# The first tile's output projection split into high and low weight parts, with the convolution's norm between them

## The chip, the cores and the metric

The kernel runs on one core of one Trainium2 chip. The core has five engines with instruction streams of their own: PE (TensorE, matmuls and transposes), DVE (VectorE), ACT (ScalarE), POOL (GpSimd) and SP (SyncE, which here only issues DMAs). They wait for one another by semaphores. Each engine takes its instructions in the order in which the built program lists them. The metric is the device time of one execution in microseconds.

## The reference, cut to what matters

Two decoder layers over 256 positions of width 1024. Each layer is a half-step SwiGLU block, a pair of token mixers side by side, and a second half-step SwiGLU block, each between two RMS norms. All is float32. The mixer pair of layer 0, on which the change acts, is

```python
proj = h @ w_in                                   # 1024 -> q, k, v, ga, gb of 512 each
q, k, v, ga, gb = jnp.split(proj, ...)
o_a = moba_attention(rope(q), rope(k), v)         # causal softmax attention here
hconv = ga * jax.nn.sigmoid(gb)
hconv = depthwise_causal_conv(hconv, conv_w, 31) + conv_b
mu = mean(hconv, -1); var = mean((hconv - mu) ** 2, -1)
o_b = silu((hconv - mu) * rsqrt(var + 1e-5) * ln_g + ln_b)
m = jnp.concatenate([o_a, o_b], -1) @ w_out       # 1024 -> 1024
x = x + rmsnorm(m, g[3])
f = swiglu(rmsnorm(x, g[4]), ffn_w_gate[layer, 1], ...)
```

Layer 1 has a gated mixer and a stick-breaking attention in the same place, with an input projection of the same kind.

## The kernel before, in words

**Tiles.** The 256 positions are two tiles of 128 (t = 0, 1). Activations that enter a matmul are transposed, so that the channel is the partition; weights move through PE in pieces of 128 rows by 512 columns.

**High and low parts.** PE multiplies a rounded form of float32 (F32R). To keep float32's accuracy every operand is two parts: ACT copies it rounded (the high part, L106 for weights, L167 for activations), and DVE subtracts that from the original (the low part, L107, L168). A product is three matmuls (`mm3`, L155 to L157): high by high, the activation's high by the weight's low, the activation's low by the weight's high. Weight blocks of 1 MB are loaded by SP into one of five buffers (`raw`, L88) and split into nine buffers each for high and low (`hi`, `lo`). A `raw` buffer is free for the next load once its second low part is made; a `hi` or `lo` buffer once the last matmul has read it.

**Scheduler.** The kernel is traced in program order, and a list scheduler then sets each engine's order, by readiness in its own model and by program order as priority. `tc.issue_after(ins)` ties instructions of a block behind `ins` on its engine. The list `fence` holds such anchors for the weight splits (L97 to L100).

**The mixer of layer 0** (`even_mixer`). Ten projections `ab` run over chunks and tiles (`turns`). The convolution's 31 taps run on POOL (0 to 12, `side_taps`) and DVE (13 to 30, `conv`, L620, into PSUM) beside the attention, and L623 adds both sums into `cacc`. `conv_norm` is a chain over all engines: PE means over channels (`cmean`, L628), DVE centres (L629), ACT squares (`csq`, L631), PE sums (`cvar`, L635), DVE and POOL make the inverse root (L637, L638), DVE puts it on a diagonal (`dg`, L642), PE spreads it (`crstd`, L644), DVE scales (L645), ACT applies silu (L649) and rounds (`xh_oT`, L651), DVE makes the low part (`xl_oT`, L652). The output projection has two halves of the weights' rows: `out_part(t, 0)` takes rows 0 to 511 (blocks `abo0`, `abo1`) with the attention's output, `out_part(t, 1)` takes `abo2`, `abo3` with the convolution's. Each is 24 matmuls into `m_t_0` and `m_t_1`. The program order is `conv`, `out_part(0, 0)`, `conv_norm` (tied behind the last matmul of it), `out_part(1, 0)`, `out_part(0, 1)`, `out_part(1, 1)`.

**After it.** When a tile's `m` is complete its `tail` runs: ACT squares it (`j_l0f`, L256), DVE and POOL make the factor, DVE updates `x` (L263), ACT squares and scales `x` (L201, `y_l0f`, L212), PE transposes (`xT_l0f`), DVE multiplies by the gain (`a_l0f`, L216), ACT and DVE split it, and the SwiGLU's first products (`gu`) follow. The SwiGLU then runs in blocks (`M`, L366 to L368) whose first DVE step (L390) subtracts two loaded blocks `raw_b`.

**The norm ahead of a mixer** (`pre_norm`). For t = 1 it gives back a function: the sums of squares come at once, but the transposes `xT`, the gain (L231) and the split come only when the first projection of tile 1 calls it (`in_proj`).

Of the kernel before, what the change touches and what calls it, by code (L numbers as in the profile page):

```python
# [49 lines left out]
def trunk(ctx, tc, x, norm_g, w_gate, w_up, w_down, ab_in, ab_out, conv_w, conv_b, conv_g, conv_bb,  # L50
# [170 lines left out]
    def pre_norm(t, gi, name):  # L221

        s = sp.tile([P, 2], F32, tag="rs", name=f"s2_{name}{t}", bufs=4)

        def parts():
            hi, lo = xT_tiles(t, name) if gi else [sp.tile([P, KD, P], F32R, tag=tag, name=f"{tag}_{name}{t}", bufs=1) for tag in (("S1", "S2"), ("S3", "tg"))[t]]
            for j in range(2):
                ps = transposes(xs[t][:, j * 512:(j + 1) * 512], f"xT{j}_{name}{t}")
                y = sp.tile([P, 512], F32, tag="y", name=f"y{j}_{name}{t}", bufs=2)
                gk = gT[:, gi * KD + 4 * j:gi * KD + 4 * j + 4, None].to_broadcast([P, 4, P])  # L230
                nc.vector.tensor_tensor(y.rearrange("p (a b) -> p a b", b=P), ps.rearrange("p (a b) -> p a b", b=P), gk, op=ALU.mult)  # L231
                split(y, hi[:, 4 * j:4 * j + 4].rearrange("p a b -> p (a b)"), lo[:, 4 * j:4 * j + 4].rearrange("p a b -> p (a b)"))
            return hi, lo

        def rstd():
            for j in range(2):
                c = slice(j * 512, (j + 1) * 512)
                junk = sp.tile([P, 512], F32, tag="y", name=f"j2{j}_{name}{t}", bufs=2)
                nc.scalar.activation(junk, xs[t][:, c], AF.Square, scale=PRE_SCALE, accum_out=s[:, j:j + 1])
            return rstd_of(s, 1e-6, f"p{name}{t}")  # L240
# [754 lines left out]
```

## Time and profile before

| | us |
|---|---|
| runs | 993.72, 995.27, 996.56 |
| median | 995.27 |
| the profiled execution | 995.27 |
| its span, first to last instruction | 993.5 |
| PE busy | 958.0 (96%) |
| PE weight loads busy | 764.0 (77%) |
| DVE busy | 829.0 (83%) |
| ACT busy | 582.6 (59%) |

The profiled execution has the time of the median, so a sum against it is a sum against the median; 1.8 us lie outside its span. All times below are microseconds from the span's start. A row of a timeline gives the start, the length from the first to the last of its instructions, the engine, the line, the output and the inputs, and in brackets how long the engine had been idle before it and what ended that. Matmuls overlap, so the distance from one start to the next is what one costs. The granted clock is a share of 2.4 GHz; 0.50 is the lower level, 1.2 GHz.

### The profile page before, as it was taken

The page shows a single profiled execution, that of the slowest core. Times are in us where ns is not written, and L with a number is a line of the kernel's source. Part 1 is how long each engine was busy: PE and PEld are TensorE (multiplying, and loading weights), DVE is VectorE, ACT ScalarE, POOL GpSimd, SP SyncE. Part 2 cuts the span into 40 slices and gives each one's busy share as a digit, 9 for nine tenths or more (in the row PEclk, how much of TensorE's full clock was granted, in tenths as well). Part 3 has the DMA queues.
Part 4 walks back from the last instruction along what each step waited for, and adds up shares of the span by engine and source line. Part 5 has one row for each costly group of instructions (what it writes and reads, how often), then busy time and mean ns, then how long its engine had stood idle before and what let it go on. Part 6 is the DMA issues. An engine that isn't in the chain of part 4 may idle for free.

```text
span 993.5 us, 11867 instructions
## 1 busy us (share of the span) xinstructions
PE 958.0 (96%) x4357; PEld 764.0 (77%) x4358; DVE 829.0 (83%) x1014; ACT 582.6 (59%) x863; POOL 91.0 (9%) x97
## 2 busy tenths in 40 slices
PE   7999999999978899999999999999999999999997
PEld 5777888778756688888777878877787778788875
DVE  6999999679867699999788999996657479999983
ACT  7575656557525566566575755565555477647561
POOL 0100000039930000000000000000000010000000
PEclk9999999999979999999999999999999999999999
DMA  9656657447015328393862566485565042749241
GB/s 316 220 175 219 205 177 274 159 146 268 1 58 187 96 85 280 127 314 99 304 211 86 171 210 224 157 294 173 170 233 169 18 153 85 222 160 302 90 180 43
DMA packets 121755, 175.33 MB, mean 176 GB/s; under 512 B 4481, under 2 KB 96321, under 8 KB 121696
## 3 DMA queue, kind: packets, MB, share of 16 engines
q1 hardware_dynamic: 121536, 174.50, 52.9%
q8 instruction: 34, 0.56, 0.2%
q14 instruction: 25, 0.20, 0.1%
q10 hardware_dynamic: 160, 0.07, 0.0%
HBM read 173.50 MB, written 1.05 MB: 176 GB/s over the span
## 4 chain that ended last, share of the span: by engine, by line
PE 81%; DVE 9%; ACT 3%; DMA 3%; issue 2%; POOL 1%; SPq 0%; POOLq 0%; DVEq 0%; ACTq 0%
PE f L155 7%; PE f L157 7%; PE f L156 7%; PE gu L155 6%; PE gu L157 6%; PE gu L156 6%; PE gX L366 4%; PE gX L367 4%; PE gX L368 4%; PE gY L366 3%; PE gY L367 3%; PE gY L368 3%; PE ab L155 2%; DVE lo_gu L107 2%; PE ab L157 2%
## 5 line engine op out<-in xcount | busy, mean ns | idle before, releaser
L155 PE MATMUL f<-hi_dn,hs 128*128 128x512 f32 x352 | 139.9, 402 | 1.6 <-ACT hs L167 1.4
L156 PE MATMUL f<-lo_dn,hs 128*128 128x512 f32 x352 | 138.3, 393 | 0.5 <-DVE lo_dn L107 0.5
L157 PE MATMUL f<-hi_dn,hs 128*128 128x512 f32 x352 | 138.0, 393 | 0.4 <-DVE hs L168 0.4
L106 ACT ACTIVATE hi_t<-raw_b 128x1024 fp32r<-128x1024 f32 x96 | 98.0, 1054 | 67.0 <-DVE raw_b L406 49.1
L107 DVE TENSOR_TENSOR lo_t<-raw_b,hi_t 128x1024 fp32r<-128x1024 f32 x96 | 114.2, 1220 | 14.6 <-ACT hi_t L106 14.6
L106 ACT ACTIVATE hi_dn<-raw_dn 128x1024 fp32r<-128x1024 f32 x88 | 91.2, 1055 | 35.3 <-PE gu L157 18.0
L107 DVE TENSOR_TENSOR lo_dn<-raw_dn,hi_dn 128x1024 fp32r<-128x1024 f32 x88 | 105.7, 1219 | 5.7 <-ACT hi_dn L106 5.5
L107 DVE TENSOR_TENSOR lo_gu<-raw_gu,hi_gu 128x1024 fp32r<-128x1024 f32 x80 | 96.1, 1219 | 9.7 <-ACT hi_gu L106 9.6
L106 ACT ACTIVATE hi_gu<-raw_gu 128x1024 fp32r<-128x1024 f32 x80 | 83.3, 1054 | 19.0 <-DMA raw_gu<-in_ffn_w_up_dram 5.0
L107 DVE TENSOR_TENSOR lo_b<-raw_b,hi_b 128x1024 fp32r<-128x1024 f32 x72 | 86.4, 1219 | 1.1 <-ACT hi_b L106 1.1
L106 ACT ACTIVATE hi_b<-raw_b 128x1024 fp32r<-128x1024 f32 x72 | 74.0, 1054 | 20.0 <-PE gu L157 15.1
L155 PEld LDWEIGHTS f<-hi_dn,hs 128*128 128x128 f32 x352 | 65.6, 188 | 18.2 <-ACT hs L167 5.4
L157 PEld LDWEIGHTS f<-hi_dn,hs 128*128 128x128 f32 x352 | 66.1, 188 | 15.9 <-DVE hs L168 2.5
L156 PEld LDWEIGHTS f<-lo_dn,hs 128*128 128x128 f32 x352 | 66.2, 188 | 15.2 <-DVE lo_dn L107 2.7
L167 ACT ACTIVATE hs<-hT 128x256 fp32r<-128x256 f32 x88 | 32.4, 379 | 66.1 <-PE hT L163 66.0
L155 PE MATMUL gu<-hi_gu,xh_l1f 128*128 128x512 f32 x160 | 63.2, 396 | 0.0
L156 PE MATMUL gu<-lo_gu,xh_l1f 128*128 128x512 f32 x160 | 62.7, 392 | 0.2 <-DVE lo_gu L107 0.2
L157 PE MATMUL gu<-hi_gu,xl_l1f 128*128 128x512 f32 x160 | 61.7, 391 | 0.6 <-DVE xl_l1f L168 0.6
L168 DVE TENSOR_TENSOR hs<-hT,hs 128x256 fp32r<-128x256 f32 x88 | 36.1, 419 | 17.2 <-ACT hs L167 16.6
L366 PE MATMUL gY<-hi_t,S 128*128 128x512 f32 x96 | 38.7, 403 | 0.0
L368 PE MATMUL gY<-hi_t,S 128*128 128x512 f32 x96 | 37.9, 395 | 0.0
L367 PE MATMUL gY<-lo_t,S 128*128 128x512 f32 x96 | 37.8, 394 | 0.0
(365 smaller groups left out, 2222.8 us busy)
## 6 DMA issues: line engine op xcount, KB each, us to landing
raw_dn<-in_ffn_w_down_dram SPq DMA_DIRECT2D x44, 1024.0 KB, 5.1
raw_b<-in_ffn_w_gate_dram SPq DMA_DIRECT2D x48, 512.0 KB, 4.2
raw_b<-in_ffn_w_up_dram SPq DMA_DIRECT2D x48, 512.0 KB, 5.7
raw_gu<-in_ffn_w_gate_dram SPq DMA_DIRECT2D x38, 512.0 KB, 4.0
raw_gu<-in_ffn_w_up_dram SPq DMA_DIRECT2D x38, 512.0 KB, 5.1
raw_ab<-in_ab_w_in_dram SPq DMA_DIRECT2D x10, 1024.0 KB, 7.0
raw_cd<-in_cd_w_in_dram SPq DMA_DIRECT2D x10, 1024.0 KB, 5.2
raw_abo<-in_ab_w_out_dram SPq DMA_DIRECT2D x4, 1024.0 KB, 5.1
```

What stands on the lines that cost most here:

```text
L106: nc.scalar.activation(hi, r, AF.Copy)
L107: nc.vector.tensor_tensor(lo, r, f32v(hi), op=ALU.subtract)
L155: nc.tensor.matmul(ps, xh, wh, start=first, stop=False)
L156: nc.tensor.matmul(ps, xh, wl, start=False, stop=False)
L157: return nc.tensor.matmul(ps, xl, wh, start=False, stop=last)
L167: nc.scalar.activation(hi, ps, AF.Copy)
L168: nc.vector.tensor_tensor(lo, ps, f32v(hi), op=ALU.subtract)
L366: nc.tensor.matmul(ps, A[0][:, k, :], wh[:, o], start=first and k == 0, stop=False, **tc_skip)
L367: nc.tensor.matmul(ps, A[0][:, k, :], wl[:, o], start=False, stop=False, **tc_skip)
L368: nc.tensor.matmul(ps, A[1][:, k, :], wh[:, o], start=False, stop=k == 3, **tc_skip)
```

## The change

Three edits. First, `out_part(0, 0)` loads `abo1` with its high parts only, multiplies all four weight pieces of rows 0 to 511 by their high parts (16 matmuls, both activation parts), then traces `conv_norm` tied behind the last of these, then makes the low parts of `abo1` tied behind the centring, and last multiplies by the low parts (8 matmuls). Second, the fence for the splits that follow is the centring at once, and for the splits of the next block it is the last rounding and the last low part of `conv_norm`. Third, `pre_norm` of tile 1 does all its work where it is called, in both layers.

```diff
+    def low_parts(raw, units):
+        with ExitStack() as stack:
+            for ins in fence:
+                stack.enter_context(tc.issue_after(ins))
+            for u, (hi, lo) in enumerate(units):
+                nc.vector.tensor_tensor(lo, raw[:, u * 1024:(u + 1) * 1024], f32v(hi), op=ALU.subtract)
...
             nc.scalar.activation(hi, r, AF.Copy)
-            nc.vector.tensor_tensor(lo, r, f32v(hi), op=ALU.subtract)
+            if low:
+                nc.vector.tensor_tensor(lo, r, f32v(hi), op=ALU.subtract)
             units.append((hi, lo))
-        return units
+        return units if low else (raw, units)
...
-        if t and gi:
-            r = rstd()
-            return lambda: (*parts(), r, None)
-        two = parts()
-        return *two, rstd(), None
+        return hi, lo, rstd_of(s, 1e-6, f"p{name}{t}"), None
...
-                if t == 1:
-                    fence[:] = [scaled.ins, last.ins]
...
-                nc.vector.tensor_tensor(ol[:, 4:8, :], cacc[:, :, o], f32v(oh[:, 4:8, :]), op=ALU.subtract)
+                low = nc.vector.tensor_tensor(ol[:, 4:8, :], cacc[:, :, o], f32v(oh[:, 4:8, :]), op=ALU.subtract)
+            late[:] = [last.ins, low.ins]
...
-            for i in (0, 1) if part == 0 else (2, 3):
+            rows = (0, 1) if part == 0 else (2, 3)
+            for i in rows:
                 if i not in ow:
-                    ow[i] = prep_rows(ab_out[0], 256 * i, f"abo{i}")
-                last = rows_product(t, accs[t], oT[t][0], oT[t][1], (2 * i, 2 * i + 1), ow[i], i == 0, i == 3)
+                    ow[i] = prep_rows(ab_out[0], 256 * i, f"abo{i}", (t, part, i) != (0, 0, 1))
+            if (t, part) == (0, 0):
+                for low in (False, True):
+                    for i in rows:
+                        for j in range(2):
+                            o = slice(j * 512, (j + 1) * 512)
+                            for k in (0, 1):
+                                wh, wl = (ow[i] if low or i == 0 else ow[i][1])[k]
+                                xh, xl = oT[t][0][:, 2 * i + k, :], oT[t][1][:, 2 * i + k, :]
+                                for a, b in ((xh, wl),) if low else ((xh, wh), (xl, wh)):
+                                    ins = nc.tensor.matmul(accs[t][j], a, b[:, o], start=not low and i + k == 0 and a is xh, stop=False)
+                    if not low:
+                        with tc.issue_after(ins.ins):
+                            fence[:] = [conv_norm().ins]
+                        low_parts(*ow[1])
+                        ow[1] = ow[1][1]
+                return
+            for i in rows:
+                rows_product(t, accs[t], oT[t][0], oT[t][1], (2 * i, 2 * i + 1), ow[i], i == 0, i == 3)
...
         conv()
-        with tc.issue_after(out_part(0, 0).ins):
-            centred = conv_norm()
+        out_part(0, 0)
         out_part(1, 0)
-        late = fence[:]
-        fence[:] = [centred.ins]
         out_part(0, 1)
         fence[:] = late
         out_part(1, 1)
```

The scheduler's orders show it. Names carry buffer numbers here, and line numbers of the changed kernel are some nine higher up to the norm (L164 to L166 are `mm3`, L703 the new loop). In names such as `m0_0_1` the last two figures are the tile and the column half, and `lo1_abo0` is the second low part of block `abo0`.

PE around the mean of `conv_norm`, before:

```order
L156 MATMUL m0_0_0_2599<-lo1_abo1_2630,xh0_oT_2254 128x512
L157 MATMUL m0_0_0_2599<-hi1_abo1_2629,xl0_oT_2255 128x512
L157 MATMUL m0_0_1_2600<-hi0_abo1_2625,xl0_oT_2255 128x512
L155 MATMUL m0_0_1_2600<-hi1_abo1_2629,xh0_oT_2254 128x512
L156 MATMUL m0_0_1_2600<-lo1_abo1_2630,xh0_oT_2254 128x512
L157 MATMUL m0_0_1_2600<-hi1_abo1_2629,xl0_oT_2255 128x512
L628 MATMUL cmean_2645<-cacc_1802,cst_69 128x256 x4
L156 MATMUL m0_1_0_2687<-lo0_abo0_2604,xh1_oT_2343 128x512
L157 MATMUL m0_1_0_2687<-hi0_abo0_2603,xl1_oT_2344 128x512
L155 MATMUL m0_1_0_2687<-hi1_abo0_2607,xh1_oT_2343 128x512
```

The same place after:

```order
L703 MATMUL m0_0_1_2600<-hi0_abo1_2613,xl0_oT_2255 128x512
L703 MATMUL m0_0_1_2600<-hi1_abo1_2616,xh0_oT_2254 128x512
L703 MATMUL m0_0_1_2600<-hi1_abo1_2616,xl0_oT_2255 128x512
L164 MATMUL m0_1_0_2687<-hi0_abo0_2603,xh1_oT_2343 128x512
L164 MATMUL m0_1_1_2688<-hi0_abo0_2603,xh1_oT_2343 128x512
L624 MATMUL cmean_2635<-cacc_1822,cst_69 128x256 x4
L703 MATMUL m0_0_0_2599<-lo0_abo0_2604,xh0_oT_2254 128x512
L703 MATMUL m0_0_1_2600<-lo0_abo0_2604,xh0_oT_2254 128x512
L165 MATMUL m0_1_0_2687<-lo0_abo0_2604,xh1_oT_2343 128x512
L166 MATMUL m0_1_0_2687<-hi0_abo0_2603,xl1_oT_2344 128x512
L164 MATMUL m0_1_0_2687<-hi1_abo0_2607,xh1_oT_2343 128x512
```

Before, the mean stands behind all 24 matmuls of tile 0 and three of tile 1. Now it stands behind the 16 high-part matmuls and two of tile 1; eight of the 16 stand further up, among the last steps of the attention, and the eight low-part matmuls follow behind the mean, mixed with those of tile 1.

DVE from the end of the convolution to the diagonal, before:

```order
L623 TENSOR_TENSOR cacc_1802<-conv1_2524,cside_1803 128x512
L107 TENSOR_TENSOR lo0_abo0_2604<-raw_abo0_2601,hi0_abo0_2603 128x1024
L107 TENSOR_TENSOR lo1_abo0_2608<-raw_abo0_2601,hi1_abo0_2607 128x1024
L107 TENSOR_TENSOR lo0_abo1_2626<-raw_abo1_2623,hi0_abo1_2625 128x1024
L107 TENSOR_TENSOR lo1_abo1_2630<-raw_abo1_2623,hi1_abo1_2629 128x1024
L629 TENSOR_TENSOR cacc_1802<-cacc_1802,cmean_2645 128x1024
L107 TENSOR_TENSOR lo0_abo2_2716<-raw_abo2_2713,hi0_abo2_2715 128x1024
L107 TENSOR_TENSOR lo1_abo2_2720<-raw_abo2_2713,hi1_abo2_2719 128x1024
L637 TENSOR_SCALAR cv4_2662<-cvar_2653 128x2
L107 TENSOR_TENSOR lo0_abo3_2738<-raw_abo3_2735,hi0_abo3_2737 128x1024
```

The same place after:

```order
L619 TENSOR_TENSOR cacc_1822<-conv1_2524,cside_1823 128x512
L116 TENSOR_TENSOR lo0_abo0_2604<-raw_abo0_2601,hi0_abo0_2603 128x1024
L116 TENSOR_TENSOR lo1_abo0_2608<-raw_abo0_2601,hi1_abo0_2607 128x1024
L625 TENSOR_TENSOR cacc_1822<-cacc_1822,cmean_2635 128x1024
L106 TENSOR_TENSOR lo0_abo1_2614<-raw_abo1_2611,hi0_abo1_2613 128x1024
L106 TENSOR_TENSOR lo1_abo1_2617<-raw_abo1_2611,hi1_abo1_2616 128x1024
L633 TENSOR_SCALAR cv4_2652<-cvar_2643 128x2
L116 TENSOR_TENSOR lo0_abo2_2716<-raw_abo2_2713,hi0_abo2_2715 128x1024
L638 TENSOR_SCALAR dg0_2655<-cst_69,cv4_2652 128x128
L638 TENSOR_SCALAR dg1_2666<-cst_69,cv4_2652 128x128
L116 TENSOR_TENSOR lo1_abo2_2720<-raw_abo2_2713,hi1_abo2_2719 128x1024
L641 TENSOR_TENSOR cacc_1822<-cacc_1822,crstd0_2657 128x4x128
```

Before, four low parts stand ahead of the centring; now two, and those of `abo1` stand behind it. All later low parts have moved down by two places in the chain: those of `abo3` now stand behind the scaling (the rows after the last one shown).

PE at the start of the mixer of layer 0, where tile 1's first projection begins, before:

```order
L156 MATMUL ab_0_1_1871<-lo1_ab_3_1_1868,xh0_l0m_1664 128x512
L157 MATMUL ab_0_1_1871<-hi1_ab_3_1_1867,xl0_l0m_1665 128x512
L163 MATMUL hcT0_1898<-cst_69,hc0_1896 128x128 x4
L163 MATMUL xT0_l0m1_1906<-cst_69,x1_68 128x128 x4
L163 MATMUL xT1_l0m1_1915<-cst_69,x1_68 128x128 x4
L155 MATMUL ab_1_0_1924<-hi0_ab_4_0_1806,xh1_l0m_1904 128x512
L156 MATMUL ab_1_0_1924<-lo0_ab_4_0_1807,xh1_l0m_1904 128x512
```

And after, where the transposes `xT0` and `xT1` of tile 1 now stand:

```order
L166 MATMUL ab_0_0_1844<-hi0_ab_4_1_1836,xl0_l0m_1665 128x512
L172 MATMUL xT0_l0m1_1778<-cst_69,x1_68 128x128 x4
L164 MATMUL ab_0_0_1844<-hi1_ab_4_1_1840,xh0_l0m_1664 128x512
L172 MATMUL xT1_l0m1_1787<-cst_69,x1_68 128x128 x4
L165 MATMUL ab_0_0_1844<-lo1_ab_4_1_1841,xh0_l0m_1664 128x512
L166 MATMUL ab_0_0_1844<-hi1_ab_4_1_1840,xl0_l0m_1665 128x512
L164 MATMUL ab_0_0_1844<-hi1_ab_4_1_1840,xh0_l0m_1664 128x512
L165 MATMUL ab_0_0_1844<-lo1_ab_4_1_1841,xh0_l0m_1664 128x512
L166 MATMUL ab_0_0_1844<-hi1_ab_4_1_1840,xl0_l0m_1665 128x512
L916 MATMUL cwT_ps_1803<-cst_69,cw_sb_584 128x31 x4
L917 MATMUL cwT_ps_1803<-cst_69,cv_sb_586 128x12
```

Before, both transposes stand between the last matmul of tile 0's second projection and the first one of tile 1. Now they stand inside tile 0's first projection, and the transposes of the small weights, which stood ahead of it, follow it. Layer 1 has the same move.

## Rows read from the trace of the kernel before

**Rows 1.** The page: the span, then busy us, share and count by engine.

```profile
span 993.5 us, 11867 instructions
...
PE 958.0 (96%) x4357; PEld 764.0 (77%) x4358; DVE 829.0 (83%) x1014; ACT 582.6 (59%) x863; POOL 91.0 (9%) x97
```

**Rows 2.** Stretches: bounds, length, busy us by engine, granted TensorE clock, DMA share, GB/s.

```profile
213.10:216.80 3.70, 2.00 (x14) 1.35 (x13) 2.02 (x3) 1.23 (x2) 1.18 (x2) 1.00 0.00 0
285.50:295.00 9.50, 6.52 (x16) 4.52 (x17) 8.43 (x12) 0.60 (x1) 0.00 (x0) 0.50 0.11 33
311.20:324.40 13.20, 13.07 (x48) 10.02 (x48) 11.68 (x14) 11.16 (x21) 0.54 (x1) 0.87 0.58 198
329.40:345.00 15.60, 15.50 (x66) 12.60 (x67) 7.89 (x13) 4.87 (x11) 0.84 (x2) 0.89 0.13 43
345.00:495.00 150.00, 149.92 (x671) 121.40 (x670) 138.78 (x149) 92.17 (x123) 0.00 (x0) 1.00 0.61 200
707.60:711.50 3.90, 2.11 (x15) 1.40 (x14) 1.98 (x4) 1.32 (x2) 0.00 (x0) 1.00 0.00 0
```

**Rows 3.** PE in order of time: start, length, instruction, idle before it and its releaser.

```profile
281.11 1.10 PE L574 MATMUL po<-va,pts 128*128 128x64 f32 x8 [0.75 <-ACT pts L571]
...
284.02 1.19 PE L574 MATMUL po<-va,pts 128*128 128x64 f32 x8 [1.36 <-ACT pts L571]
...
285.99 1.11 PE L163 MATMUL oT<-cst,o 128*128 128x128 f32 x4 [0.79 <-DVE o L582]
...
291.24 0.80 PE L156 MATMUL m<-lo_abo,xh_oT 128*128 128x512 f32 x1 [2.23 <-DVE lo_abo L107]
...
298.19 1.89 PE L628 MATMUL cmean<-cacc,cst 128*128 128x256 f32 x8
...
302.55 1.95 PE L635 MATMUL cvar<-cst,csq 128*128 128x1 f32 x16
...
306.95 0.60 PE L644 MATMUL crstd<-dg,cst 128*128 128x128 f32 x4
...
311.28 0.50 PE L155 MATMUL m<-hi_abo,xh_oT 128*128 128x512 f32 x1 [3.72 <-ACT xh_oT L651]
...
326.78 1.27 PE L163 MATMUL xT_l0f<-cst,y_l0f 128*128 128x128 f32 x8 [2.43 <-ACT y_l0f L212]
...
329.40 0.79 PE L155 MATMUL gu<-hi_gu,xh_l0f 128*128 128x512 f32 x1 [1.36 <-ACT xh_l0f L167]
...
344.81 0.48 PE L155 MATMUL gu<-hi_gu,xh_l0f 128*128 128x512 f32 x1
```

**Rows 4.** DVE in order of time, the same columns.

```profile
288.77 1.28 DVE L623 TENSOR_TENSOR cacc<-conv,cside 128x512 f32<-128x512 f32 x2
...
289.97 4.62 DVE L107 TENSOR_TENSOR lo_abo<-raw_abo,hi_abo 128x1024 fp32r<-128x1024 f32 x4
...
300.12 1.22 DVE L629 TENSOR_TENSOR cacc<-cacc,cmean 128x1024 f32<-128x1024 f32 x1 [5.53 <-PE cmean L628]
...
307.96 1.28 DVE L645 TENSOR_TENSOR cacc<-cacc,crstd 128x512 f32<-128x512 f32 x2
...
332.72 2.29 DVE L390 TENSOR_TENSOR raw_b<-raw_b,raw_b 128x2048 f32<-128x2048 f32 x1
...
699.77 1.41 DVE L263 SCALAR_TENSOR_TENSOR x<-tg_l1m,v_ql1m,x 128x512 f32<-128x512 f32 x2
```

**Rows 5.** ACT in order of time.

```profile
301.43 1.07 ACT L631 ACTIVATE csq<-cacc 128x1024 f32<-128x1024 f32 x1 [13.69 <-DVE cacc L629]
...
318.94 0.60 ACT L256 ACTIVATE j_l0f<-m 128x512 f32<-128x512 f32 x1 [0.68 <-PE m L157]
...
325.07 1.04 ACT L106 ACTIVATE hi_dn<-raw_dn 128x1024 fp32r<-128x1024 f32 x1
```

**Rows 6.** SP's queue of DMA issues in order of time.

```profile
326.87 0.50 SPq L88 DMA_DIRECT2D raw_b<-in_ffn_w_up_dram  x1
...
353.63 19.40 SPq L88 DMA_DIRECT2D raw_dn<-in_ffn_w_down_dram  x2
```

More of the change, by code (lines that the diff above doesn't have):

```diff
@@ L78, in trunk, with prep @@
     nc.scalar.activation(early, mhalf, AF.Silu)
-    def prep(loads, name):
-        return split_raw(load(loads, name), name)
+    def prep(loads, name, low=True):
+        return split_raw(load(loads, name), name, low)
     def load(loads, name):
@@ L91, in trunk, with split_raw @@
     fence = []
-    def split_raw(raw, name):
+    def split_raw(raw, name, low=True):
         with ExitStack() as stack:
@@ L97, in split_raw, with split_raw_now @@
                 stack.enter_context(tc.issue_after(ins))
-            return split_raw_now(raw, name)
-    def split_raw_now(raw, name):
+            return split_raw_now(raw, name, low)
+    def low_parts(raw, units):
[4 more added lines that the diff above has]
+                nc.vector.tensor_tensor(lo, raw[:, u * 1024:(u + 1) * 1024], f32v(hi), op=ALU.subtract)
+    def split_raw_now(raw, name, low=True):
         units = []
@@ L146, in prep_in, with prep_rows @@
         return [(hi[:, o:o + 512], lo[:, o:o + 512]) for hi, lo in units for o in (0, 512)]
-    def prep_rows(w, r0, name):
+    def prep_rows(w, r0, name, low=True):
         def loads(raw):
@@ L151, in loads @@
             return [(v, w[r0:r0 + 256, :].rearrange("(k p) f -> p k f", p=P))]
-        return prep(loads, name)
+        return prep(loads, name, low)
     def mm3(ps, xh, xl, wh, wl, first, last):
@@ L223, in pre_norm @@
         s = sp.tile([P, 2], F32, tag="rs", name=f"s2_{name}{t}", bufs=4)
[L225 to L240, printed above, removed]
-        if t and gi:
-            r = rstd()
-            return lambda: (*parts(), r, None)
-        two = parts()
-        return *two, rstd(), None
+        hi, lo = xT_tiles(t, name) if gi else [sp.tile([P, KD, P], F32R, tag=tag, name=f"{tag}_{name}{t}", bufs=1) for tag in (("S1", "S2"), ("S3", "tg"))[t]]
@@ new lines, in pre_norm @@
+        for j in range(2):
+            ps = transposes(xs[t][:, j * 512:(j + 1) * 512], f"xT{j}_{name}{t}")
+            y = sp.tile([P, 512], F32, tag="y", name=f"y{j}_{name}{t}", bufs=2)
+            gk = gT[:, gi * KD + 4 * j:gi * KD + 4 * j + 4, None].to_broadcast([P, 4, P])
+            nc.vector.tensor_tensor(y.rearrange("p (a b) -> p a b", b=P), ps.rearrange("p (a b) -> p a b", b=P), gk, op=ALU.mult)
+            split(y, hi[:, 4 * j:4 * j + 4].rearrange("p a b -> p (a b)"), lo[:, 4 * j:4 * j + 4].rearrange("p a b -> p (a b)"))
@@ L248, in post_norm @@
+        for j in range(2):
+            c = slice(j * 512, (j + 1) * 512)
+            junk = sp.tile([P, 512], F32, tag="y", name=f"j2{j}_{name}{t}", bufs=2)
+            nc.scalar.activation(junk, xs[t][:, c], AF.Square, scale=PRE_SCALE, accum_out=s[:, j:j + 1])
+        return hi, lo, rstd_of(s, 1e-6, f"p{name}{t}"), None
     def post_norm(t, acc, g, half, name, last=False):
@@ L495, in in_proj @@
     def in_proj(t, c, units, pre, name):
-        if callable(pre[t]):
-            pre[t] = pre[t]()
         hi, lo = pre[t][0:2]
@@ L644, in conv_norm @@
                 nc.tensor.matmul(pb[:, 0:P], ones, dg, start=True, stop=True)
-                scaled = nc.vector.tensor_tensor(cacc[:, :, o], cacc[:, :, o], pb[:, None, 0:P].to_broadcast([P, 4, P]), op=ALU.mult)
-                if t == 1:
-                    fence[:] = [scaled.ins, last.ins]
+                nc.vector.tensor_tensor(cacc[:, :, o], cacc[:, :, o], pb[:, None, 0:P].to_broadcast([P, 4, P]), op=ALU.mult)
                 for i in range(4):
@@ L680, in even_mixer @@
         ow = {}
+        late = []
         def proj(t, ci):
@@ L692, in out_part @@
                 accs[t] = [ps_acc(f"m0_{t}_{i}", 0) if t == 0 else ps_mm(f"m0_{t}_{i}") for i in range(2)]
-            for i in (0, 1) if part == 0 else (2, 3):
+            rows = (0, 1) if part == 0 else (2, 3)
+            for i in rows:
                 if i not in ow:
-                    ow[i] = prep_rows(ab_out[0], 256 * i, f"abo{i}")
-                last = rows_product(t, accs[t], oT[t][0], oT[t][1], (2 * i, 2 * i + 1), ow[i], i == 0, i == 3)
+                    ow[i] = prep_rows(ab_out[0], 256 * i, f"abo{i}", (t, part, i) != (0, 0, 1))
+            if (t, part) == (0, 0):
+                for low in (False, True):
+                    for i in rows:
+                        for j in range(2):
+                            o = slice(j * 512, (j + 1) * 512)
[12 more added lines that the diff above has]
+                rows_product(t, accs[t], oT[t][0], oT[t][1], (2 * i, 2 * i + 1), ow[i], i == 0, i == 3)
             if part == 1:
                 tail(t, accs[t])
-            return last
         rest = None
```

## The prediction

> **What bounds the kernel now.** I read the page first [rows 1]. PE is busy for 958.0 of 993.5 us, the engine next to it, DVE, for 829.0. PE's idle time is therefore 993.5 - 958.0 = 35.5 us in all, and a change that leaves the number and size of the matmuls alone, as this one does, can gain only from that idle time and from stretches at the lower clock.
>
> Next I read stretches [rows 2]. In the middle of a SwiGLU (345 to 495 us) PE is busy 149.92 of 150.00 us at a clock of 1.00, and a matmul costs 149.92 / 671 = 0.224 us. DVE is busy 138.78 there and so has 11.2 us to spare. In such a stretch PE is the bound, and a head start won ahead of it is carried to the end. Around the convolution's norm it is otherwise: from 285.5 to 295.0 PE is busy for 6.52 of 9.50 us at a clock of 0.50, the lower level, and a matmul row costs 6.52 / 16 = 0.41 us.
>
> Third, PE in order of time tells what it waits for [rows 3]: 0.75 and 1.36 us for the softmax's `pts`, 0.79 for `o`, 2.23 for `lo_abo`, 3.72 for the rounded output of the norm (`xh_oT`), 2.43 for `y_l0f`, 1.36 for `xh_l0f`. The first five are 8.85 us, and a reader should see what they hide: `cacc` is ready at 288.77 + 1.28 = 290.05 [rows 4], yet `cmean` starts at 298.19 [rows 3], 8.1 us later, only because all 24 matmuls of the first half stand ahead of it, and these wait for low parts that DVE makes in 4 x 1.155 us from 289.97 on. ACT idles 13.69 us before `csq` for the same reason [rows 5].
>
> The profiled execution took 995.27 us, the median of the runs, so the sum is made against that (993.5 of span and 1.8 around it).
>
> **The change, part by part.**
>
> *Term 1, tile 1's norm in layer 0.* The transposes `xT0`, `xT1` move in among the matmuls of the first projection. From 213.10 to 216.80 PE is busy for 2.00 of 3.70 us [rows 2], so 1.70 goes if nothing else is late. Tile 1's `x` is old by then, and the gain and the split lie beside some 18 projection matmuls (18 x 0.224 = 4.0 us). The convolution's side taps may start later for it; at worst that moves `cacc` and eats the gain. Bounds 0 and 1.7, and I take -1.7, since every instruction whose wait is removed has its inputs early.
>
> *Term 2, the same in layer 1.* Idle is 3.90 - 2.11 = 1.79 [rows 2]. Here `x` is fresh: its two updates end at 699.77 + 1.41 = 701.2 [rows 4], the half that `xT0` wants some 0.7 sooner, and the moved transposes may wait about 0.4 for it. I take -1.4 (bounds 0 and 1.8).
>
> *Term 3, the projection around the norm.* Eight of the sixteen high-part matmuls now stand inside the attention's last steps, where they fill the waits of 0.75 and 1.36. The wait of 2.23 for `lo_abo` disappears, as high parts need no DVE. `cmean` waits for `cacc` alone: 290.05 instead of 298.19. Then DVE: `lo0_abo0`, `lo1_abo0` stand ahead of the centring and end at 289.97 + 2 x 1.155 = 292.28, while `cmean` is done at 290.05 + 1.89 = 291.94, so the centring starts at 292.3, 0.3 late. `csq` follows after 1.31 (301.43 - 300.12), at 293.6, and `cvar` could start 1.12 after it (302.55 - 301.43), at 294.7. But PE has 15 matmuls between: 291.94 + 15 x 0.224 = 295.3, which is later and so counts. From `cvar` to `crstd` 4.40 and from there to the matmul with `xh_oT` 4.33, as before [rows 3]: 304.0 instead of 311.28, thus -7.2. One low part (1.155) now stands between diagonal and scaling; it fits nearly into the 1.01 (307.96 - 306.95) that DVE waits there anyway.
>
> What is late next is again `xh_oT`: of the 8.85 us some 1.6 stay, up to 3.0 if PE runs its matmuls faster than before. The low parts of `abo1` end at 292.3 + 1.22 + 2 x 1.155 = 295.8 instead of 289.97 + 4.62 = 294.6, and SP's next load into that buffer starts 1.2 later; it holds a block of the SwiGLU, which PE reaches some 25 us after that. Bounds of the term: 5.0, if the clock is at half up to about 291.7 as in the row, so that ten matmuls cost 0.41 instead of 0.224 (1.9 us) and the centring's delay is not caught up; 7.5 with all 0.3 of it caught up.
>
> The Trainium skill, "Perfetto Trace Analysis", section "Matmul Optimizations", says that TensorE scales its power with its use, so that matmuls should run back to back in batches. The row agrees in so far as the clock is 0.50 behind the waits of 0.75, 1.36 and 0.79 [rows 2, 3]. By that rule the eight matmuls packed into these waits would keep the clock up, and the term stays at 7.2; if the row's 0.50 comes back all the same, it is 5.0 and the sum below 986.2.
>
> *Term 4, the tail.* From `j_l0f` at 318.94 [rows 5] to `xT_l0f` at 326.78 [rows 3] the first tile's chain takes 7.84 us, of which PE waits for 2.43. By the new fences one copy with its low part fewer stands in the chain's way on ACT (1.04, as `hi_dn` at 325.07 [rows 5]) and about one on DVE (1.155, of which I count 0.65, as it lies partly beside POOL's step). That is -1.7; bounds 0 and 2.4.
>
> *Term 5.* That work doesn't vanish; a quarter of a low part ends up between `xT_l0f` and the first `gu`, whose wait was 1.36: +0.3 (0 to 0.4).
>
> *Term 6, a new wait.* On DVE the first SwiGLU step L390 now stands between the first tile's last steps and those of tile 1. It needs a block `raw_b` whose load was issued at 326.87 [rows 6], once a low part of `gu` had freed the buffer. That low part has moved back in DVE's order by about as much as the path moves ahead, so I keep 326.9. L390 started at 332.72 [rows 4], so the load lands within 5.85 of its issue, and L390's 2.29 end by 335.0. Behind it queue three short steps, of about 0.5 each (an estimate from the 0.6 to 0.7 that halves of 128 x 512 take in [rows 4]), that lead to tile 1's first `gu`: 336.5. Without the wait it would be 344.81 [rows 3] - 7.2 - 1.7 + 0.3 = 336.2. So +0.3 to +0.4, and I take 0.4. By these terms 8.2 are left at this point.
>
> *Clock.* From 311.20 to 324.40 48 matmuls took 13.07 us at 0.87 [rows 2], 48 x 0.224 = 10.75 at full clock: 2.3 lost. Whether the shorter wait for `xh_oT` still brings the clock down I can't tell: 2.3 either way, value 0. Small new waits in the SwiGLU: value 0, bound 1.5 worse.
>
> Sum: 1.7 + 1.4 + 7.2 + 1.7 - 0.3 - 0.4 = 11.3; 995.3 - 11.3 = 984.0.
>
> **The rivals.**
>
> *Half of it.* The clock stays at 0.50 around the norm (term 3 is 5.0) and the tail's chain is paced by something other than the copies (term 4 is 0): 1.7 + 1.4 + 5.0 - 0.3 - 0.4 = 7.4, so 987.9. For it: the stretch at 0.50 and 0.87 [rows 2]. Against: the moved matmuls fill the very waits ahead of it.
>
> *DVE paces the SwiGLU.* Whatever PE wins ahead of it is given back inside, because DVE has as much to do as before; only the mixers' terms, or the one in layer 1, stay: 1.4 to 3.1, so 992.2 to 993.9. Against it: DVE's 138.78 beside PE's 149.92 in 150 us [rows 2]. For it: PE's weight loads (764.0) are less busy than DVE (829.0) [rows 1]. The Trainium skill, "Perfetto Trace Analysis", section "Identifying the Most-Contended Engine", speaks for this rival: TensorE's matmul time says little, its weight loads' busy share is to be read, so 77% against DVE's 83%, and DVE would be the engine to relieve. The trace here doesn't bear it out in the SwiGLU's stretch, where PE never waits.
>
> *The norm isn't earlier.* `cacc` or the centring moves back with the steps that now stand ahead on DVE or POOL, and the wait for `xh_oT` grows by what that for `lo_abo` loses: terms 1 and 2 remain, 992.2. Against it: `cacc` at 290.05 hangs on nothing that was moved behind it.
>
> *The load behind L390 comes late (slower).* If its issue on SP stands behind another that waits, as the one at 353.63 waited 19.40 [rows 6], it goes out at 326.9 + 19.4 = 346.3, lands at 352.1, L390 ends at 354.4, and tile 1's `gu` starts near 356, 11 later than before; with terms 1 and 2 that is +8, 1003. The whole change turns into a loss once the block lands after 344.81 + 3.1 - 2.29 - 1.5 = 344.1. For it: three DVE steps are blocked by one load, and its buffer is freed later in the order. Against it: in the trace of before that load waited only 0.50 on the queue.
>
> **How the numbers follow.** Forecast 0.64, half of it 0.16, DVE 0.08, norm not earlier 0.04, late load 0.08. A difference under 0.3% (3 us) is about what a measurement of this kernel can't tell from none. The first two are faster (0.80), the next two count as the same (0.12), the last is slower (0.08). Low end: all bounds at their best, 1.7 + 1.8 + 7.5 + 2.4 + 2.3 (clock) - 0.4 = 15.3, 980.0. High end: the rival with half of it, 987.9, made worse by the 1.5 in the SwiGLU and 2.1 of the clock's 2.3, 991.5. Outside lie the last three cases, 0.20.
>
> **What would show it.** Right: `cmean` about 8 us earlier and waiting for `cacc`; no wait for `lo_abo`; one wait of 1.6 to 3 for `xh_oT`, near 304; `xT_l0f` waiting under 1; tile 1's `gu` near 336; no waits in the two mixers' places; PE as busy in the SwiGLU as before. Wrong: more than 14 us from `cmean` to the matmul with `xh_oT`, idle PE inside the SwiGLU, or a wait of over 2 us that ends with L390.

## The result and the profile after

| | before | after |
|---|---|---|
| median of the runs, us | 995.91 | 982.67 |
| ratio, 95% interval | | 0.9871 [0.9852, 0.9889] |
| the profiled execution | 995.27 | 983.43 |
| its span | 993.5 | 981.6 |

By the ratio the change takes 12.8 us (11.1 to 14.7) off 995.9; forecast were 984.0 and 11.3. The page after, beside [rows 1]:

```profile
span 981.6 us, 11876 instructions
...
PE 954.6 (97%) x4358; PEld 763.6 (78%) x4358; DVE 829.2 (84%) x1014; ACT 581.5 (59%) x863; POOL 91.8 (9%) x97
```

PE's idle time fell from 35.5 to 981.6 - 954.6 = 27.0 us; the other 3.4 us of the span are busy time. 2.3 of that lie between the front and the restart with `xh_oT` (68.84 to 66.53), where the granted clock rose from 0.93 to 0.97. DVE works as long as before. Stretches of the changed kernel, with the columns of [rows 2]; the first is the mixer's front, the second the same piece of the SwiGLU as before:

```profile
201.81:231.87 30.06, 30.06 (x144) 24.43 (x142) 24.19 (x30) 17.47 (x24) 15.39 (x14) 1.00 0.60 207
...
345.00:495.00 150.00, 149.92 (x671) 121.18 (x670) 134.80 (x145) 91.52 (x125) 0.54 (x1) 1.00 0.61 200
```

The front has no idle time left, and in the SwiGLU PE is as full as it was: 149.92 us, 671 matmuls. PE around the norm, beside [rows 3]:

```profile
282.87 1.10 PE L570 MATMUL po<-va,pts 128*128 128x64 f32 x8 [0.89 <-ACT pts L567]
284.75 0.66 PE L172 MATMUL oT<-cst,o 128*128 128x128 f32 x4 [0.78 <-DVE o L578]
...
289.13 1.89 PE L624 MATMUL cmean<-cacc,cst 128*128 128x256 f32 x8
...
294.29 1.84 PE L631 MATMUL cvar<-cst,csq 128*128 128x1 f32 x16
...
298.86 0.61 PE L640 MATMUL crstd<-dg,cst 128*128 128x128 f32 x4
...
302.91 0.79 PE L164 MATMUL m<-hi_abo,xh_oT 128*128 128x512 f32 x1 [2.75 <-ACT xh_oT L645]
...
317.00 1.27 PE L172 MATMUL xT_l0f<-cst,y_l0f 128*128 128x128 f32 x8 [1.51 <-ACT y_l0f L221]
319.65 0.79 PE L164 MATMUL gu<-hi_gu,xh_l0f 128*128 128x512 f32 x1 [1.38 <-ACT xh_l0f L176]
...
334.50 0.74 PE L166 MATMUL f<-hi_dn,hs 128*128 128x512 f32 x2 [0.20 <-DVE hs L177]
```

The wait of 0.75 for `pts` and the one of 2.23 for `lo_abo` are gone, those for `pts` (1.36), `xh_oT` (3.72) and `y_l0f` (2.43) are smaller. DVE, beside [rows 4], and POOL, of which [rows 1] give only the sum:

```profile
287.07 1.28 DVE L619 TENSOR_TENSOR cacc<-conv,cside 128x512 f32<-128x512 f32 x2
288.27 2.35 DVE L116 TENSOR_TENSOR lo_abo<-raw_abo,hi_abo 128x1024 fp32r<-128x1024 f32 x2
291.06 1.22 DVE L625 TENSOR_TENSOR cacc<-cacc,cmean 128x1024 f32<-128x1024 f32 x1 [0.44 <-PE cmean L624]
...
314.45 0.21 DVE L200 TENSOR_SCALAR v_pl0f<-s_l0f 128x1 f32<-128x1 f32 x1
314.58 2.35 DVE L116 TENSOR_TENSOR lo_gu<-raw_gu,hi_gu 128x1024 fp32r<-128x1024 f32 x2
...
331.49 2.29 DVE L388 TENSOR_TENSOR raw_b<-raw_b,raw_b 128x2048 f32<-128x2048 f32 x1 [2.27 <-DMA raw_b<-in_ffn_w_up_dram]
```

```profile
311.26 0.54 POOL L201 TENSOR_TENSOR v_ql0f<-v_ql0f,mhalf 128x1 f32<-128x1 f32 x1 [13.24 <-DVE v_ql0f L200]
314.74 1.46 POOL L201 TENSOR_TENSOR v_pl0f<-v_pl0f,mhalf 128x1 f32<-128x1 f32 x1 [2.93 <-DVE v_pl0f L200]
...
324.53 2.59 POOL L201 TENSOR_TENSOR v_pl0f<-v_pl0f,mhalf 128x1 f32<-128x1 f32 x1 [2.79 <-DVE v_pl0f L200]
```

The two low parts stand ahead of the centring, which then waits 0.44 us for PE instead of 5.53. POOL's power step (the inverse root, L201), the same operation on one column, takes 0.54, 1.46 or 2.59 us. It became the point of the second half of the study.

Single executions differ by a few us, so each stage was measured in every trace, as the distance from one marked PE row to the next (us). The marks are `xT_l0m` of tile 0, the second `hcT`, `cmean`, the restart with `xh_oT`, the first and the last `xT_l0f`, the first `xT_l1f`, `xT_l1m`, the first `xT_l1f` behind layer 1's mixer, and the last matmul:

| | front | to cmean | to restart | to xT_l0f | tile 1's xT | SwiGLU | next SwiGLU | layer 1's mixer | last SwiGLU |
|---|---|---|---|---|---|---|---|---|---|
| before | 42.69 | 64.95 | 13.09 | 15.50 | 17.57 | 162.58 | 178.92 | 115.24 | 185.63 |
| before, again | 42.67 | 65.18 | 13.09 | 15.50 | 17.64 | 162.60 | 178.12 | 113.84 | 184.71 |
| after | 40.36 | 57.26 | 13.78 | 14.09 | 18.07 | 163.18 | 179.22 | 112.15 | 184.58 |
| after, again | 40.36 | 55.94 | 13.89 | 12.71 | 18.15 | 163.18 | 178.97 | 112.20 | 184.72 |
| norm early only | 40.38 | 66.41 | 13.08 | 16.02 | 17.64 | 162.65 | 177.89 | 111.84 | 184.65 |
| projection only | 42.71 | 57.09 | 13.78 | 12.69 | 17.69 | 163.20 | 177.70 | 113.85 | 184.63 |
| quarters | 40.34 | 55.96 | 12.41 | 15.53 | 18.80 | 163.17 | 178.45 | 111.82 | 184.74 |
| last version | 40.36 | 55.94 | 12.42 | 12.41 | 17.72 | 164.10 | 178.03 | 111.89 | 184.69 |

Where two kernels share code and waits, most columns repeat to 0.1 us; "next SwiGLU", where no edit acts, differs by up to 1.5 (by 0.8 between the two executions of the kernel before), so differences of that size there are taken as chance.

### The profile page after: what moved, and what is told of

Read it like the earlier page. It is cut to its first block, busy times and chain, and to the rows that moved or that the text cites. A ratio compares the mean times of both kernels' runs of the same rounds, so it can differ in the third digit from the quotient of the medians.

```text
span 981.6 us, 11876 instructions
## 1 busy us (share of the span) xinstructions
PE 954.6 (97%) x4358; PEld 763.6 (78%) x4358; DVE 829.2 (84%) x1014; ACT 581.5 (59%) x863; POOL 91.8 (9%) x97
## 4 chain that ended last, share of the span: by engine, by line
PE 78%; DVE 10%; DMA 4%; ACT 4%; issue 2%; POOL 1%; SPq 0%; POOLq 0%; DVEq 0%; ACTq 0%
PE f L164 7%; PE f L165 7%; PE f L166 7%; PE gu L166 5%; PE gu L164 5%; PE gu L165 5%; PE gX L365 4%; PE gX L364 4%; PE gX L366 4%; PE gY L364 3%; PE gY L365 3%; PE gY L366 3%; PE ab L164 2%; PE ab L166 2%; PE ab L165 2%; PE hT L172 2%
## 5 line engine op out<-in xcount | busy, mean ns | idle before, releaser
L164 PE MATMUL f<-hi_dn,hs 128*128 128x512 f32 x352 | 140.4, 402 | 0.8 <-ACT hs L176 0.5
L166 PE MATMUL f<-hi_dn,hs 128*128 128x512 f32 x352 | 137.9, 394 | 0.4 <-DVE hs L177 0.4
L164 PEld LDWEIGHTS f<-hi_dn,hs 128*128 128x128 f32 x352 | 65.7, 188 | 17.6 <-ACT hs L176 4.9
L166 PEld LDWEIGHTS f<-hi_dn,hs 128*128 128x128 f32 x352 | 66.1, 188 | 16.2 <-DVE hs L177 2.9
L165 PEld LDWEIGHTS f<-lo_dn,hs 128*128 128x128 f32 x352 | 66.3, 188 | 14.7 <-DVE lo_dn L116 2.3
L164 PE MATMUL gu<-hi_gu,xh_l1f 128*128 128x512 f32 x160 | 63.3, 397 | 0.0
L166 PE MATMUL gu<-hi_gu,xl_l1f 128*128 128x512 f32 x160 | 61.8, 391 | 0.6 <-DVE xl_l1f L177 0.6
```

The lines of the kernel that those rows point to most:

```text
L164: nc.tensor.matmul(ps, xh, wh, start=first, stop=False)
L165: nc.tensor.matmul(ps, xh, wl, start=False, stop=False)
L166: return nc.tensor.matmul(ps, xl, wh, start=False, stop=last)
```

## The experiments

**Each part alone.** The first kernel is the old one with the third edit alone, the second the changed one without it:

```diff
...
-        if t and gi:
-            r = rstd()
-            return lambda: (*parts(), r, None)
...
```

> The kernel before with the third edit alone (tile 1's norm ahead of the mixers at once, both layers). Theory: each mixer's wait goes, and the head start is carried to the end; the traces of before and after gave 2.3 us in layer 0 and 2.0 in layer 1, so about 991.5 (4 us under before), with no wait for hcT, hpad, tk_kT, skT on PE. The prediction's own terms 1 and 2 would give 992.2. Rival, DVE paces what follows: the layer 0 part is given back before the end of the convolution on DVE, and about 994 is left.

> The changed kernel with tile 1's old deferred norm: the projection's split alone. Theory: terms 3 to 6 are independent of the mixers' fronts, so 8 us under before, about 987; cmean some 8 us earlier against the attention's end, one wait of 2.5 to 3 for xh_oT. Rival: the parts lean on one another (the convolution on DVE ends earlier only because layer 0's front is shorter), then under 6 us are gained, 990 or more.

Measured: 0.9960 [0.9947, 0.9973], 4.0 us, and 0.9922 [0.9907, 0.9938], 7.8 us, as both theories said. The sum, 11.8, lies within the whole change's 11.1 to 14.7, so the parts add up within that. The table places them: 2.3 in the front, 1.7 in layer 1's mixer (113.85 to 112.15), the rest around the norm. With the norm alone, 2.3 were won in the front and 1.2 to 1.5 lost again up to `cmean`, but not to waits for DVE: PE's idle time in that column is 5.48 us with and without the edit. The last `po` and 12 matmuls ran at half clock there, where the kernel before had 8 and 10 such matmuls in its two traces:

```profile
281.84 1.97 PE L561 MATMUL po<-va,pts 128*128 128x64 f32 x8 [1.37 <-ACT pts L558]
```

**Where the norm stands.** First it was put behind all 24 matmuls, high parts still first; then the old order of products was kept and the norm tied behind the first 12:

```diff
                     if not low:
-                        with tc.issue_after(ins.ins):
-                            fence[:] = [conv_norm().ins]
                         low_parts(*ow[1])
                         ow[1] = ow[1][1]
+                with tc.issue_after(ins.ins):
+                    fence[:] = [conv_norm().ins]
```

```diff
...
+                last = rows_product(t, accs[t], oT[t][0], oT[t][1], (2 * i, 2 * i + 1), ow[i], i == 0, i == 3)
+                if (t, i) == (0, 0):
+                    with tc.issue_after(last.ins):
+                        fence[:] = [conv_norm().ins]
```

> The changed kernel with high parts first, but the norm traced and tied behind all 24 matmuls of tile 0's first half, low parts of abo1 at once. Theory: what counts is where the norm stands; cmean comes some 5 us later than in the changed kernel (near 294), few matmuls are left to lie beside the chain, the restart with xh_oT is near 307 instead of 302.9, and the time is about 987. Rival: high parts first alone does it, since they fill the attention's waits and remove that for lo_abo: 983 to 984.

> The changed kernel with the old product order (high, low, low per piece) and the norm tied behind the first 12 matmuls, those of abo0; abo1 behind the centring. Theory: cmean must wait for the two low parts of abo0, 2 us later than in the changed kernel, and the attention's waits stay unfilled; the restart comes about 2 us later, 985. Rival 1: only that the norm stands early counts: 983. Rival 2: all 16 high-part matmuls are needed to cover the chain: 988 or more.

Measured: 0.9940 [0.9929, 0.9952] and 0.9937 [0.9924, 0.9950], 6.9 and 6.6 us behind the full change. That high parts first, or an early norm, would do alone is refuted. The theory was right on the first in kind, but too mild on both: their restarts come 5.6 and 5.7 us late (117.01 and 117.07 us after `xT_l0m`, in the changed kernel 111.40), where some 4 and 2 were expected. PE in the first kernel, then in the second:

```profile
292.55 1.89 PE L624 MATMUL cmean<-cacc,cst 128*128 128x256 f32 x8
296.91 1.95 PE L631 MATMUL cvar<-cst,csq 128*128 128x1 f32 x16
301.21 1.20 PE L640 MATMUL crstd<-dg,cst 128*128 128x128 f32 x4 [2.02 <-DVE dg L638]
305.63 0.80 PE L164 MATMUL m<-hi_abo,xh_oT 128*128 128x512 f32 x1 [3.22 <-ACT xh_oT L645]
```

```profile
290.12 0.80 PE L165 MATMUL m<-lo_abo,xh_oT 128*128 128x512 f32 x1 [2.22 <-DVE lo_abo L116]
...
294.55 2.31 PE L624 MATMUL cmean<-cacc,cst 128*128 128x256 f32 x8
299.33 1.95 PE L631 MATMUL cvar<-cst,csq 128*128 128x1 f32 x16
304.01 0.61 PE L640 MATMUL crstd<-dg,cst 128*128 128x128 f32 x4
308.07 0.50 PE L164 MATMUL m<-hi_abo,xh_oT 128*128 128x512 f32 x1 [0.93 <-ACT xh_oT L645]
```

In the first the matmuls are used up before the chain ends, and two waits of 2.02 and 3.22 take their place. In the second the chain is covered (0.93 left, so rival 2 had the size but not the cause), but `cmean` comes as late as in the first: PE had stood still ahead of it for `lo_abo` (2.22 us) and `pts` (0.75 and 1.36), and ran at half clock behind that.

**The clock behind a wait.** The same kernel again, and one with idle products in the wait for `xh_oT`:

```diff
-                nc.tensor.matmul(pb[:, 0:P], ones, dg, start=True, stop=True)
+                spread = nc.tensor.matmul(pb[:, 0:P], ones, dg, start=True, stop=True)
+                if t == 0:
+                    with tc.issue_after(spread.ins):
+                        for n in range(14):
+                            nc.tensor.matmul(pvr[:, 128:512], zb[:, 0:P], zb[:, 0:384], start=True, stop=True)
```

> The changed kernel once more, beside the three below. Theory: the stretches at half clock behind the waits differ from execution to execution (12 to 29 matmuls between 285 and 330 us in the profiles so far), so this profile shows the same waits (2.8 for xh_oT, 1.5 for xT_l0f, 1.4 for gu) and another length at 0.50, some 1 to 2 us apart. Rival: the lengths belong to the program, and this profile repeats 7, 6 and 7 matmuls at 0.43 us.

> The changed kernel with 14 idle products of 128 x 384 (zeros, into a part of PSUM that nothing reads) between the first crstd and the restart with xh_oT. They use only time in which PE waits. Theory: the half clock behind the restart comes from the wait, so with PE busy in it the 6 matmuls at 0.43 us become 0.23, 1.2 us gained there and about 1 us in the time. Rival: the clock falls all the same, or the products push the restart back: no gain, or up to 1 us slower.

Measured: 0.9869 [0.9851, 0.9887] and 0.9872 [0.9853, 0.9891]. The stretch of 3.5 us behind the same wait, in the first and the second trace of the changed kernel:

```profile
302.90:306.40 3.50, 3.49 (x9) 2.83 (x10) 2.28 (x4) 3.47 (x6) 0.00 (x0) 0.57 1.06 337
```

```profile
303.00:306.50 3.50, 3.47 (x15) 2.84 (x16) 2.27 (x4) 3.47 (x6) 0.00 (x0) 1.00 1.04 324
```

9 rows against 15, at 0.57 and 1.00, with the wait the same to 0.04 us: the clock behind this wait differs between two executions of one program, which is worth 1.4 us in the column to `xT_l0f`. What went before differed too: in the first, the granted clock was 0.56 over the matmuls ahead of `cmean` (285.2 to 289.1), in the second 1.00. Behind the wait for `xh_l0f` (1.38 us in both) both ran 7 matmuls at half clock. The filled wait brought nothing in the time. PE ran at full clock behind it, but so did the kernel without filling, so it settles nothing on that. It showed something else:

```profile
300.27 0.50 PE L164 MATMUL m<-hi_abo,xh_oT 128*128 128x512 f32 x1 [0.25 <-ACT xh_oT L649]
...
315.08 1.27 PE L172 MATMUL xT_l0f<-cst,y_l0f 128*128 128x128 f32 x8 [3.41 <-ACT y_l0f L221]
```

PE did its 48 matmuls without a pause and then waited longer, 3.41 instead of 1.52 us: the tail's chain, in which POOL's power took 2.59 us here instead of 1.46, now sets the end of this stage.

**A shorter chain to the restart.** Tile 0's output is rounded in quarters; the second kernel also has five idle products ahead of the first `gu`:

```diff
+                step = 1 if t == 0 else 4
+                for a in range(0, 4, step):
+                    for i in range(a, a + step):
...
+                    last = nc.scalar.activation(oh[:, 4 + a:4 + a + step, :], cacc[:, a:a + step, o], AF.Copy)
...
```

```diff
+            if (name, t, j) == ("l0f1", 0, 1):
+                fill(turned[0], 5, "spare5")
```

> The changed kernel, but for tile 0 each quarter of the norm's output is rounded and its low part made as soon as its silu is done, instead of after all four. Theory: PE waits for the ACT chain; its first matmul needs one quarter only, so the restart comes 1.5 to 2 us earlier, the wait for xh_oT falls from 2.8 to about 1, and 1.5 us or a little more is gained. Rival: the eight small steps on ACT and DVE cost as much as they bring (PE then waits for the second or third quarter), under 0.5 us.

> Quarters as in the run before, and five idle products of 128 x 512 between xT_l0f and the first gu. Theory: the 7 matmuls at 0.43 us behind that wait run at 0.23, 1.4 us more than the quarters alone, about 3 us under the changed kernel. Rival: the wait of 1.5 us ahead of xT_l0f is what brings the clock down, and the five products run at half clock themselves: nothing beyond the quarters, or some tenths lost.

Measured: 0.9867 [0.9852, 0.9881] and 0.9869 [0.9849, 0.9889], no gain in either. The first theory held for its step (the wait for `xh_oT` fell from 2.8 to 1.29) and failed for the time, by a third cause. PE, then DVE and POOL, of the first:

```profile
299.44 0.50 PE L164 MATMUL m<-hi_abo,xh_oT 128*128 128x512 f32 x1 [1.29 <-ACT xh_oT L647]
...
314.97 1.97 PE L172 MATMUL xT_l0f<-cst,y_l0f 128*128 128x128 f32 x8 [4.33 <-ACT y_l0f L221]
```

```profile
311.41 2.35 DVE L116 TENSOR_TENSOR lo_gu<-raw_gu,hi_gu 128x1024 fp32r<-128x1024 f32 x2
311.57 2.59 POOL L201 TENSOR_TENSOR v_pl0f<-v_pl0f,mhalf 128x1 f32<-128x1 f32 x1 [3.92 <-DVE v_pl0f L200]
```

All that was won turned into the wait for `y_l0f`, and 2.59 of that chain is one power on POOL, beside which DVE makes two low parts. In the second kernel the rival came out: the idle products ran at half clock themselves (0.43 us apart, granted clock 0.50 from 316.4 to 320.9). The `gu` behind them soon ran at 0.23 us each, and 0.6 us were won up to tile 1's last `xT_l0f` (18.17 where the quarters alone have 18.80), too little to show in the time.

**DVE kept quiet beside POOL.** DVE copies POOL's result, and low parts are tied behind the copy: those of the second block with the changed kernel, the same with the quarters, and with the quarters also the second half of the first block:

```diff
+            if (name, t) == ("l0f1", 0):
+                seen = sp.tile([P, 1], F32, tag="seen", name="seen", bufs=1)
+                guard[:] = [nc.vector.tensor_copy(seen, r).ins]
...
+                if (l, j, c) == (0, 1, 1):
+                    fence.extend(guard)
```

> The changed kernel, and DVE reads the result of POOL's power step (a copy of one column) right behind v_pl0f of tile 0; the low parts of the SwiGLU's second block are tied behind that copy. DVE so runs no low part while POOL works. Theory: POOL's step lasts 0.54 us alone and 1.46 or 2.59 beside one or two low parts on DVE, and it holds up xT_l0f; here it takes 0.54, PE's wait for y_l0f falls from 1.5 to 0.6, and up to 1 us is gained. Rival: the length of that step is only a matter of when it was recorded, and y_l0f starts as late as before: no difference.

> The same beside the rounding in quarters, where POOL's step took 2.59 us and PE waited 4.33 for y_l0f. Theory: 0.54 instead of 2.59, so the wait falls to about 2.3, and 2 us more than the quarters alone are gained, about 980 where the changed kernel has 982. Rival: no difference.

> As the run before, and the low parts of the second half of the SwiGLU's first block stand behind the copy too, so v_pl0f no longer waits for two of them (2.35 us). Theory: the tail's chain is what holds PE now; y_l0f comes 3 us earlier than with the quarters alone, the wait for it falls from 4.33 to about 1.2, 978 to 979. Rival: the low parts are then late themselves, and PE waits for lo_gu or for the gained a_l0f in the first products of the SwiGLU: 981 or more.

Measured: 0.9848 [0.9828, 0.9868], 0.9846 [0.9827, 0.9864], 0.9840 [0.9820, 0.9861]. POOL and PE of the first, then PE of the second and of the third:

```profile
310.45 0.54 POOL L201 TENSOR_TENSOR v_pl0f<-v_pl0f,mhalf 128x1 f32<-128x1 f32 x1 [2.87 <-DVE v_pl0f L200]
```

```profile
311.81 1.27 PE L172 MATMUL xT_l0f<-cst,y_l0f 128*128 128x128 f32 x8 [0.61 <-ACT y_l0f L226]
314.81 0.50 PE L164 MATMUL gu<-hi_gu,xh_l0f 128*128 128x512 f32 x1 [1.74 <-ACT xh_l0f L176]
```

```profile
313.49 1.97 PE L172 MATMUL xT_l0f<-cst,y_l0f 128*128 128x128 f32 x8 [2.28 <-ACT y_l0f L226]
```

```profile
311.49 1.27 PE L175 MATMUL xT_l0f<-cst,y_l0f 128*128 128x128 f32 x8 [1.20 <-ACT y_l0f L227]
314.47 0.50 PE L167 MATMUL gu<-hi_gu,xh_l0f 128*128 128x512 f32 x1 [1.71 <-ACT xh_l0f L179]
...
325.55 0.50 PE L168 MATMUL gu<-lo_gu,xh_l0f 128*128 128x512 f32 x1 [0.59 <-DVE lo_gu L117]
```

Each wait came out as expected: 0.61, 2.28 in the second kernel, 1.20. The power takes 0.54 in all three. Of the 0.9 us won in the first some 0.35 went into the next wait, for `xh_l0f` (1.38 to 1.74). Beside the first kernel the quarters still bring nothing, as the wait for `y_l0f` takes them up: from `cmean` to `xT_l0f` it is 25.72 us in the first and 25.90 in the second; only the third, where `v_pl0f` has no low part ahead of it either, comes to 24.83. The third is the fastest version, 977.91 us where its neighbour of before had 994.38; against the changed kernel that is 0.9840 to 0.9869, whose intervals just overlap, so the traces carry the claim more than the times. It also gave 0.9 us back in the SwiGLU (164.10), where its late low parts are missed (a wait of 0.59 for `lo_gu`).

**The kernel before, again.**

> The kernel before once more, for a second trace. The first one took 115.24 us from layer 1's first transposes to its last norm, and 185.63 from there to the last matmul, where every kernel with either edit took 111.8 to 113.9 and 184.6 to 185.0. Theory: some 1.4 and 1.0 us of that are chance of that one execution (three slow matmuls at 764.7, a wait of 0.81 for hs), so this trace shows about 113.9 and 184.7. Rival: they belong to the kernel before, and the change takes them away: 115.2 and 185.6 again. The waits of 2.23, 3.72 and 2.43 us around the norm should repeat to the hundredth, the matmuls at half clock (8, 8 and 7) need not.

Measured: 113.84 and 184.71, and the waits of 2.23, 3.72 and 2.43 within 0.02 us; 10, 9 and 8 slow matmuls instead of 8, 8 and 7. This execution took 992.47 us, its neighbour 994.79. The theory holds: 1.4 us in layer 1's mixer and 0.9 at the end were chance of the first trace. They flatter the comparison of the first two profiles, whose start does the opposite (`xT_l0m` at 190.55 and 191.51, ahead of any edit).

## Why the prediction was right

The mechanism was as forecast. By the second traces (before, again; after, again) its terms read:

- *Term 1*, 1.7: measured 2.31 (42.67 to 40.36). The idle 1.70 went, and PE's 144 rows also took 0.63 less (30.69 to 30.06 us).
- *Term 2*, 1.4: measured 1.64, with the forecast wait for the fresh `x` (0.29 instead of 0.4). Within its bounds.
- *Term 3*, 7.2: measured 65.18 + 13.09 - 55.94 - 13.89 = 8.44, in the first traces 7.00. The chain from `cmean` to the restart was forecast at 304.0 - 290.05 = 14.0 and is 13.78 and 13.89. One detail holds in one trace only. In the first, `cacc` is ready at 288.35 and `cmean` waits for the ten matmuls ahead of it, part of them at half clock. In the second, at full clock, it starts as the first half of `cacc` is made (288.41 + 0.68 = 289.09), as forecast:

```profile
288.41 1.28 DVE L619 TENSOR_TENSOR cacc<-conv,cside 128x512 f32<-128x512 f32 x2
289.14 1.99 PE L624 MATMUL cmean<-cacc,cst 128*128 128x256 f32 x8
```

  The bounds of 5.0 to 7.5 were too narrow on the good side, since the clock there may also be full.
- *Term 4*, 1.7: mis-sized. PE's wait for `y_l0f` fell by 0.92 (2.43 to 1.51). The kernel before, where the low part on DVE began only after the power had:

```profile
324.99 0.54 POOL L192 TENSOR_TENSOR v_pl0f<-v_pl0f,mhalf 128x1 f32<-128x1 f32 x1 [3.93 <-DVE v_pl0f L191]
325.20 1.22 DVE L107 TENSOR_TENSOR lo_gu<-raw_gu,hi_gu 128x1024 fp32r<-128x1024 f32 x1 [0.28 <-ACT hi_gu L106]
326.02 1.32 ACT L212 ACTIVATE y_l0f<-x,v_pl0f 128x512 f32<-128x512 f32 x2
```

  POOL was done at 325.53 and `y_l0f` began at 326.02, so the copy `hi_dn` on ACT cost some 0.5 there and not the 1.04 put down for it. After the change it is out of the way, but POOL's power rose from 0.54 to 1.46, as a low part now ran beside it; keeping DVE off it brought the wait to 0.61, which is near the forecast 0.7. That the new fences moved the copy, as the prediction has it, isn't shown: no run has the old ones.
- *Term 5*, +0.3: measured nothing (1.36 to 1.38).
- *Term 6*, +0.4: measured 0.5 (17.64 to 18.15). L388 waited 2.27 us for the load, as forecast, and PE saw 0.2 of it as a wait for `hs` (334.50).
- *SwiGLU*, value 0: 0.58 is given back (162.60 to 163.18). It is so in all versions whose norm goes ahead of the block's last products (163.13 or more, also with the old order of products, 163.14), but not with the third edit alone (162.65), and hardly with the norm behind all 24 matmuls (162.79). The cause stays open.
- *Clock*, value 0: the columns to `cmean` and to `xT_l0f` differ by 1.3 and 1.4 us between two executions of one kernel, so the bound of 2.3 was of the right size. Of the 2.3 lost behind the restart before, 1.9 came back in the second trace (13.07 to 11.20 us of PE) and 0.5 in the first (12.58).

That the sum lands within 1.5 us is in part luck: by the second traces terms 1, 3 and the clock brought 3.7 more than forecast, and term 4, the SwiGLU and the stretch behind it 2.2 less.

The rival in which DVE paces the SwiGLU falls with 149.92 us of PE in the same 150 us, and with a column that grows by 0.58 where 10 to 13 us were won ahead of it. The one in which the norm isn't earlier falls with `cmean`, which comes 7.7 and 9.2 us earlier by its column. The one called half of it had the lower clock right in part for the first trace, but term 3 still gave 7.0 there, and the tail 0.9. The late load came, but as 2.27 us of DVE's time, landing near 331.5, far from the 344.1 at which it would have turned the result.

Two of the signs came out otherwise. `xT_l0f` waited 1.51 us and not under 1, which is term 4. A wait of over 2 us that ends with L390 (here L388) was named as a sign of being wrong, and DVE's 2.27 us is one; PE saw 0.2 of it, so the sign was drawn too wide.

## What to carry to other kernels

Where a chain over several engines stands beside a block of matmuls, ask what has to be ready for the first of them: products that need no slow operand go ahead, the chain starts as soon as its own input is there, and the rest lies beside it. When PE's wait is removed, look at once at the chain that ends the stage: two edits here shortened a wait by about 1.5 us and won nothing, as low parts and POOL's step held up the chain behind it. Measure by stage and in two traces before a difference of 1 to 2 us is believed.
